# A matrix product with a decayed running sum: the first and last slots planned anew, chunk 2 read in pairs, the last two blocks copied in two pieces

## The chip, the cores and the metric

The kernel runs on one core of a Trainium2 chip, in one launch. Times are microseconds of device time (us): the median of several runs, and, for everything read from inside, one execution taken by the hardware profiler. The engines are named PE (matrix products), ACT (scalar engine), DVE (vector engine), POOL (GpSimd) and SP (the engine that issues the stores).

## The reference

```python
B, S, D = (16, 2048, 1024)          # x [B,S,D], w [D,D], decay [D], all float32
xw = x @ w
out[:, 0, :] = xw[:, 0, :]
for t in range(1, S):
    out[:, t, :] = decay[None, :] * out[:, t - 1, :] + xw[:, t, :]
```

Each of the 16 sequences is multiplied by one 1024x1024 matrix, and each output channel then runs a first-order recurrence over its 2048 time steps with its own decay.

## The kernel before

**Tiling.** Time is cut into 64 chunks of 512 tokens, four per sequence. The output channels are cut into eight blocks, n = 0 to 7, of 128. Chunks are taken two at a time; a *slot* is one pair of chunks and one n, so 31 pairs give 248 slots, and the last pair is split into its two chunks and gives 16 more: 264 slots. In a slot PE computes [128 channels x 1024 times] in PSUM with sixteen matmuls of 128x512 over the eight k-blocks (L131). Slots count from 0 and, near the end, backwards from -1. PSUM tiles come from a ring `ps` of three, so slot s writes the bank that slot s-3 used, and PE must wait until the readers of slot s-3 are done; two halves, `spare` and `spare1`, help at both ends.

**Input.** x is loaded by POOL's queue in four quarter loads for each chunk (`load`, L105, deed L) into `xb` (three buffers), cast to bf16 on the way. DVE transposes each chunk in 32x32 squares of float32 words (`turn`, L115, deed T), that is of pairs of bf16, into `xw` (two buffers). ACT then copies it in two parts (`part`, L123, deeds X and Y) into `xt`, where the even and odd members of the pairs are apart, and the matmuls read xt. Where the argument `pairs` is given, a matmul reads xw directly, every second bf16 of it, and needs no X or Y. A turn also puts the four loads of the chunk three further on in the list `loads`; each L in the plan issues the next one.

**Recurrence.** A slot is treated in one of two ways.
- *Direct*: DVE scans the 1024 times out of PSUM into `so` (`run`, L221, deed S).
- *Paired*: ACT copies PSUM to `xs` (L183, p), and writes the odd step's scaled value to `h` (L169 on ps, g); POOL adds them (`join`, L196, j); DVE scans only every second time, with the squared decay (L201, S); ACT scales those results (L169 on so, h), and POOL fills in the other times (`fill`, L246, c). z prepares the column ahead of the scan.

By default a slot is paired unless n % 4 == 3; `flips` lists the slots where this is turned round. k (L250) saves the last column for the next pair of chunks. DVE then transposes the slot back (`back`, L258, deed B) into an `ot` buffer, and when four blocks n are together, SP stores them in four stores (L279).

**The order.** `pin` keeps the program order on every engine, so the order in which the deeds are written is the order in which each engine works, and an engine whose next instruction has to wait holds up all behind it. For most slots `usual` makes the deeds. For the first slots (keys 0 to 33), and for the last (negative keys), the dictionary `agenda` has them written out, one line to a slot; the letters are the deeds above. Key -99 is done before the first slot: loads of x (M) and of w (U), transposes and copies of the first two chunks (E; F on DVE, G on ACT), and the weights' casts W on DVE and w on ACT (`settle`, L302). PE's own order is fixed by the loop over slots (L537). In slots 8 and 9 the matmuls of the two slots are issued chunk by chunk (L580 to L584).

**The end.** The last four slots are not transposed back by DVE. `ending` (L371, deed V) transposes them on PE in sixteen 128x128 pieces, blocks 0 to 3 of 128 times by rows r = 0 to 3 (L383), and `leave` copies each block of four rows from PSUM (L387; ACT for blocks 0 and 2, DVE for 1 and 3) and issues one store for it (L389).

Of the kernel before, what the change touches and what calls it, by code (L numbers as in the profile page):

```python
# [14 lines left out]
def _ap(ap_obj: bass.AP, new_ap, extra_offset=0):  # L15
    return dataclasses.replace(
        ap_obj,
        ap=[list(p) for p in new_ap],
        offset=ap_obj.offset + extra_offset,
    )  # L20
# [5 lines left out]
def kernel(  # L26
# [26 lines left out]
    nc = tc.nc  # L53
    pin = tc.keep_in_program_order
    B, S, D = x.shape
    assert w.shape == (D, D)

    NQ = 4
# [7 lines left out]
    R = K // 2  # L66
# [9 lines left out]
    def ring(pool, name, count, shape, dtype=FP32):  # L76
        i = turns[name] = turns.get(name, -1) + 1
        return pool.tile(shape, dtype, name=f"{name}{i % count}")
# [19 lines left out]
    xw_of = {}  # L98
# [42 lines left out]
    class Tile:  # L141
# [39 lines left out]
        def copy(self):  # L181
            self.xs = sb.tile([128, 2 * TL], FP32, name=f"xs{self.lot % 3}")[:, 0:self.T]
            pin(nc.scalar.copy(out=self.xs, in_=self.ps))  # L183
# [141 lines left out]
    for q in range(NQ):  # L325
        pin(nc.sync.dma_start(
            out=rows[q * P:q * P + R],
            in_=_ap(decay, [[P, R], [CH, 2], [1, P]], q * CR)))
# [42 lines left out]
    def ending(i):  # L371
        b, t0 = chunks[-1]
        nb = TL // 128
        pts = [ring(psp, name, count, [128, R, 128])
               for name, count in (("spare1", 1), ("ps", 3), ("ps", 3), ("spare", 1))]
        wides = [ring(sb, *spot, [128, NQ, R, P])
                 for spot in (("xb", 3), ("xb", 3), ("xb", 3), ("h", 4))]

        def cross(blocks, rs):
            for i in blocks:  # L380
                for r in rs:
                    t = 2 + i * 128
                    pin(nc.tensor.transpose(  # L383
                        out=pts[i][:, r], in_=tiles[r - R].so[:, t:t + 128], identity=ident))

        def leave(i, copy):
            pin(copy(out=wides[i].rearrange("p q r i -> p r q i"),  # L387
                     in_=pts[i].rearrange("p r (q i) -> p r q i", q=NQ)))
            pin(nc.sync.dma_start(  # L389
                out=_ap(out, [[D, 128], [1, CH]], (b * S + t0 + i * 128) * D + CH),  # L390
                in_=wides[i].rearrange("p q r i -> p (q r i)")))

        cross((0,), range(R))
        cross((1,), range(R))
        cross((2, 3), range(R - 1))
        cross((2, 3), (R - 1,))
        for i in range(nb):
            leave(i, (nc.scalar.copy, nc.vector.tensor_copy)[i % 2])

    slots = [(g, n) for g in groups[:-1] for n in range(K)]  # L400
    slots += [([c], n) for c in groups[-1] for n in range(K)]
    tiles = []

    def turn_and_load(c):
# [4 lines left out]
    loads = [(c, q) for c in (2, 3, 4) for q in range(NQ)]  # L409
# [19 lines left out]
        "d": square_again,  # L429
        "I": identity,  # L430
        "V": ending,
        "p": lambda s: tiles[s % len(slots)].copy(),
        "g": lambda s: tiles[s % len(slots)].odd(),
# [7 lines left out]
        "L": lambda i: load(*loads.pop(0)) if loads else None,  # L441
    }
    agenda = {
        -99: "M0 M1 U0 M2 M3 U1 U2 w0 W1 w2 W3 K0 K1 K2 K3 E0 E1 G0 E2 G1 E3 F2 G3 E4 E5 G4 E6 G5 E7 F6 G7 W4 w5 W6 W7 D E8 E9 G8 E10 G9 E11 F10 G11 E12 L E13 G12 L E14 G13 E15 L F14 G15",
        0: "p0 z0 W8 W9 W10 W11",
        1: "g0",
        2: "L S1 L",
        3: "p2 z2 L g2 j0 S3 w12 w13 L w14 L w15 k1",
        4: "j2 B1 d k3",
        5: "p4 L S0 L g4 S2 L k0 h0 j4 B3 h2",  # L450
        6: "k2 c0 T2 c2 p5 g5 B0 L X2 L",
        7: "B2 L L Y2 T3 L z4 z5 j5 p6 S4 z6 L g6 L X3 S5 j6 S7 Y3 L S6 h4 k7 k5 c4 k4 h5 B7",
        8: "",
        9: "k6 h6 c5 B4",
        10: "p8 g8 c6 T4 z8 p9 j8 g9 B5 X4",
        11: "L j9 B6 p10 S8 L z9 z10 g10 S9 h8",
        12: "j10 Y4 S11 L c8 h9 T5 c9",
        13: "p12 L g12 B9 j12 X5 S10 L",
        14: "Y5 B8 L B11 h10 z12 c10 S13",
        15: "p14 L g14 S12 j14 T6 h12 L",  # L460
        16: "p15 c12 g15 B10 L X6 j15 B12",
        17: "z14 Y6 S14 L B13 z15 h14 S15 p16 z16 c14",
        18: "g16 T7 L h15 j16 p17 g17 B14 z17 c15 X7",
        19: "S16 j17 p18 B15 L g18 L S17 k16 h16 z18 j18",
        20: "Y7 S19 L c16 k17 h17 T8 k19 L c17",
        21: "p20 g20 L S18 X8 j20 B17 B19",
        22: "L h18 p21 c18 B16 k18 g21 B18 Y8 z20 L j21 S20",
        23: "p22 z21 z22 S21 L h20 g22 T9 c20 h21",
        24: "k21 k20 j22 S23 X9 L c21 Y9 B20 L",
        25: "B23 k23 p24 B21 g24 z24 j24 S22 z25",  # L470
        26: "p25 T10 k22 h22 g25 c22 S24 X10 j25",
        27: "B22 p26 S25 g26 z26 Y10 j26",
        28: "S27 h25 h24 c25 S26 c24",
        29: "B27 h26 c26 T11 p28 g28 j28 B24",
        30: "p29 B25 g29 z28 j29 S28 z29 S29",
        31: "h28 p30 c28 B26 g30 h29 B28 j30 z30",
        32: "c29 S31 S30 h30 B29 c30 p32 g32 z32 j32 B30 B31 L L",
        33: "p33 g33 z33 j33 S32 h32 c32 k32 L L",
        -20: "z-20",
        -19: "p-20 g-20",  # L480
        -18: "j-20 S-19 S-20 k-19 B-19",
        -17: "h-20 k-20 c-20 S-18 B-20 k-18",
        -16: "I S-17",
        -15: "z-15 B-18 k-17",
        -14: "p-15 g-15 B-17 z-14 j-15",
        -13: "p-14 S-16 g-14 j-14 S-15 k-16",
        -12: "S-13 h-15 k-15 c-15 S-14 k-13",
        -11: "p-12 B-13 h-14 B-15 g-12 c-14 k-14 B-16",
        -10: "j-12 B-14 z-12 S-12 z-10 S-11",
        -9: "p-10 k-12 g-10 h-12 B-11 j-10 k-11",  # L490
        -8: "S-9 c-12 S-10 k-9",
        -7: "z-7 B-12 h-10 k-10 B-9 c-10 S-8",
        -6: "p-7 g-7 B-10 j-7 B-8",
        -5: "S-7 S-6 h-7 c-7",
        -4: "z-4 S-5 B-7",
        -3: "p-4 B-6 g-4 B-5 j-4",
        -2: "S-3 S-4",
        -1: "S-2 h-4 c-4 a-1 b-1 V",
    }
    flips = (1, 13, 15, -19, -18, -16, -11, -8, -6, -3, -2)  # L500
    later = {}
    begun = {"T": 12, "X": 11, "Y": 11}
    for c in range(5, nch):
# [6 lines left out]
    def usual(s):  # L510
# [9 lines left out]
        if not paired[s - 1]:  # L520
            do.append(f"B{s - 1}")
        return do + later.get(s, []) + ["L"] * (2 if len(loads) > NQ else 1)

    def rest(s):
        do = [f"S{s - 1}"] if tiles[s - 1].paired else []
        do.append(f"C{s - 1}")
        if tiles[s - 2].paired:
            do.append(f"B{s - 2}")
        return do + [f"B{s - 1}"] + later.get(s, []) + ["L"] * len(loads)

    def perform(do):
        for deed in do:
            deeds[deed[0]](int(deed[1:] or 0))
# [3 lines left out]
    for step, (g, n) in enumerate(slots):  # L537
        T = TL * len(g)
        left = step - len(slots)
# [5 lines left out]
        if step == 0:  # L545
# [10 lines left out]
            for k0 in range(0, K, 2):  # L556
                for i in range(R):
                    for k in (k0, k0 + 1):
                        matmul(seconds[i], i, k, xt_of[1], 0, H * P,
                               pairs=xw_of[1] if k0 < 4 else None)  # L560
            for i in range(R):
                for k in range(K):
                    matmul(seconds[i], i, k, xt_of[1], H * P, TL, H * P,
                           pairs=xw_of[1] if i < 2 else None)
        if step < R:
            ps = heads[n] if n < 3 else tuple(spares)
        else:
            if step == K + 1:
                ps = nexts
            elif len(g) == 2 or n % R < 3:  # L570
                ps = ring(psp, "ps", 3, [128, T])
            else:
                ps = ring(psp, "spare", 1, [128, TL])
            todo = [(k, l) for k in range(K) for l in range(len(g))]
            if step < K:
                todo.sort(key=lambda kl: kl[0] % 2)
            elif step == K:
                todo = []
                nexts = ring(psp, "ps", 3, [128, T])
                for l in range(len(g)):  # L580
                    for i, both in enumerate((ps, nexts)):
                        for k in range(K):
                            matmul(both[:, l * TL:(l + 1) * TL], n + i, k, xt_of.get(g[l]),
                                   pairs=xw_of[g[l]] if g[l] in (3,) else None)  # L584
            elif step == K + 1:
                todo = []
            if left == -1:
                ps = tuple(both[:, t:t + TL // 2] for t, both in zip(
                    (0, TL // 2), (ps, ring(psp, "ps", 3, [128, TL]))))
                for t, half in zip((0, TL // 2), ps):  # L590
                    for k in range(K):
                        matmul(half, n, k, xt_of[g[0]], t, t + TL // 2, t)
                todo = []
            for k, l in todo:
                matmul(ps[:, l * TL:(l + 1) * TL], n, k, xt_of[g[l]])
        tiles.append(Tile(g, n, ps, outlets))
        do = agenda.get(step, agenda.get(left) if left >= -20 else None)
        if do is None:
            do = usual(step)
        else:  # L600
            do = do.split()
            if left == -20:
                do = rest(step) + do
        perform(do)
    assert not loads
# [28 lines left out]
```

## Time and profile before

| what | value |
|---|---|
| median of 4 runs | 905.81 us (905.63 to 906.38) |
| profiled execution, whole | 905.67 us |
| its span in the profile | 903.80 us |
| granted TensorE clock | 0.999 |
| PE busy, share of the span | 896.6 us, 99% |
| DVE busy | 826.1 us, 91% |
| ACT busy | 684.4 us, 76% |
| POOL busy | 655.1 us, 72% |
| paired slots | 189 of 264 |
| memory read and written | 138.42 MB and 134.22 MB, 302 GB/s over the span |

The span runs from the first to the last instruction that the profiler shows; the execution's own time is 1.87 us longer. Starts and lengths below are from this one execution and count from the start of the span. A line of the timeline has start, length, engine, line of the kernel, operation and tiles, and in brackets the idle time before it with what ended it. "L131 <- DVE so L221" in a list of waits means that the matmul of line 131 waited for the instruction of line 221 on DVE.

### The profile page before, as it was taken

The page shows a single profiled execution, that of the slowest core. Times are in us where ns is not written, and L with a number is a line of the kernel's source. Part 1 is how long each engine was busy: PE and PEld are TensorE (multiplying, and loading weights), DVE is VectorE, ACT ScalarE, POOL GpSimd, SP SyncE. Part 2 cuts the span into 40 slices and gives each one's busy share as a digit, 9 for nine tenths or more (in the row PEclk, how much of TensorE's full clock was granted, in tenths as well). Part 3 has the DMA queues.
Part 4 walks back from the last instruction along what each step waited for, and adds up shares of the span by engine and source line. Part 5 has one row for each costly group of instructions (what it writes and reads, how often), then busy time and mean ns, then how long its engine had stood idle before and what let it go on. Part 6 is the DMA issues. An engine that isn't in the chain of part 4 may idle for free.

```text
span 903.8 us, 12070 instructions
## 1 busy us (share of the span) xinstructions
PE 896.6 (99%) x4201; PEld 411.2 (45%) x4201; DVE 826.1 (91%) x628; ACT 684.4 (76%) x951; POOL 655.1 (72%) x753
## 2 busy tenths in 40 slices
PE   9999999999999999999999999999999999999997
PEld 5444444444444444444444444444444444444444
DVE  4999999999999999999998999999999999999997
ACT  4889867777877877877778778778777787787742
POOL 7888678777767768677677677787777776776622
PEclk9999999999999999999999999999999999999999
DMA  9999999999999999999999999999999999999868
GB/s 193 195 215 218 231 214 216 215 240 251 238 247 258 242 247 257 250 243 243 225 236 229 223 229 232 227 228 229 228 229 225 236 231 223 225 233 209 175 143 233
DMA packets 402543, 204.77 MB, mean 227 GB/s; under 512 B 8753, under 2 KB 401457, under 8 KB 402481
## 3 DMA queue, kind: packets, MB, share of 16 engines
q1 hardware_dynamic: 265168, 134.76, 61.1%
q0 software_dynamic: 137024, 68.70, 56.7%
q8 instruction: 33, 0.54, 0.2%
q10 hardware_dynamic: 288, 0.52, 0.2%
q14 instruction: 30, 0.24, 0.1%
HBM read 138.42 MB, written 134.22 MB: 302 GB/s over the span
## 4 chain that ended last, share of the span: by engine, by line
PE 93%; DVE 2%; DMA 2%; POOL 2%; issue 1%; ACT 1%; DVEq 0%; POOLq 0%
PE ps L131 92%; DMA xb<-in_x_dram 2%; DVE so L221 1%; POOL ot L295 1%; PE spare L131 1%; POOL xb L105 1%; ACT xt L123 0%; DVE so L201 0%; ACT xs L183 0%; DVE ot L258 0%; DVE xw L115 0%; ACT h L169 0%; POOL xs L196 0%; PE spare L383 0%; PE ps L383 0%
## 5 line engine op out<-in xcount | busy, mean ns | idle before, releaser
L131 PE MATMUL ps<-xt,wsb 128*128 128x512 bf16 x4024 | 868.0, 378 | 0.9 <-DVE wsb L302 0.5
L131 PEld LDWEIGHTS <-wsb 128*128 128x128 bf16 x4152 | 405.9, 98 | 480.4 <-issue 1.0
L196 POOL TENSOR_TENSOR xs<-h,xs 128x512 f32<-128x512 f32 (+1 forms) x189 | 241.9, 1280 | 191.2 <-ACT h L169 84.1
L183 ACT COPY xs<-ps 128x1024 f32<-128x1024 f32 (+1 forms) x189 | 188.7, 998 | 155.3 <-PE ps L131 150.7
L258 DVE STREAM_TRANSPOSE ot<-so 128x1024 f32<-128x1024 f32 (+1 forms) x260 | 300.1, 1192 | 2.9 <-POOL so L190 1.1
L246 POOL TENSOR_TENSOR so<-h,xs 128x512 f32<-128x512 f32 (+1 forms) x189 | 240.3, 1273 | 43.3 <-ACT h L169 27.8
L123 ACT COPY xt<-xw 128x2048 bf16<-128x2048 bf16 (+1 forms) x136 | 242.2, 1789 | 7.7 <-DVE xw L115 7.7
L105 POOL DMA_DIRECT2D xb<-in_x_dram x264 | 174.0, 660 | 3.3 <-DMA ot<-in_w_dram 1.1
L169 ACT ACTIVATE h<-so,dec 128x512 f32<-128x512 f32 (+1 forms) x189 | 144.7, 766 | 26.8 <-DVE so L201 23.6
L115 DVE STREAM_TRANSPOSE xw<-xb 128x2048 f32<-128x2048 f32 (+1 forms) x78 | 147.3, 1901 | 5.6 <-DMA xb<-in_x_dram 5.6
L201 DVE TENSOR_TENSOR_SCAN so<-spare,keep,xs 128x512 f32<-128x512 f32 (+1 forms) x96 | 119.4, 1245 | 27.6 <-POOL xs L196 27.3
L201 DVE TENSOR_TENSOR_SCAN so<-spare,xs 128x512 f32<-128x512 f32 x93 | 113.3, 1220 | 26.7 <-POOL xs L196 23.8
L169 ACT ACTIVATE h<-ps,dec 128x512 f32<-128x512 f32 (+1 forms) x189 | 129.6, 685 | 0.0
L221 DVE TENSOR_TENSOR_SCAN so<-dec,ps 128x1024 f32<-128x1024 f32 x34 | 76.9, 2260 | 1.0 <-ACT h L169 1.0
L221 DVE TENSOR_TENSOR_SCAN so<-dec,keep,ps 128x1024 f32<-128x1024 f32 (+1 forms) x36 | 77.2, 2145 | 0.2
L250 ACT COPY keep<-so 128x1 f32<-128x1 f32 x136 | 25.4, 189 | 13.1 <-DVE so L221 12.6
L192 ACT COPY so<-keep 128x1 f32<-128x1 f32 x96 | 18.2, 191 | 2.0 <-DVE ot L258 1.8
L131 PE MATMUL ps<-xw,wsb 128*128 128x256 bf16 (+1 forms) x68 | 11.2, 301 | 0.0
L190 POOL MEMSET so<- 128x1 f32 x93 | 10.6, 116 | 0.6 <-DVE ot L258 0.6
L131 PE MATMUL spare<-xt,wsb 128*128 128x512 bf16 (+1 forms) x48 | 10.0, 335 | 0.0
L295 POOL DMA_DIRECT2D ot<-in_w_dram x12 | 6.5, 544 | 3.1 <-DMA xb<-in_x_dram 2.0
L320 PE MATMUL spare<-idle 128*128 128x512 bf16 x22 | 6.8, 484 | 1.2 <-DVE idle L310 1.2
(37 smaller groups left out, 36.5 us busy)
## 6 DMA issues: line engine op xcount, KB each, us to landing
out_dram<-ot SPq DMA_DIRECT2D x248, 512.0 KB, 11.0
xb<-in_x_dram POOLq DMA_DIRECT2D x248, 256.0 KB, 7.8
out_dram<-ot SPq DMA_DIRECT2D x12, 256.0 KB, 4.3
xb<-in_x_dram POOLq DMA_DIRECT2D x16, 128.0 KB, 5.6
ot<-in_w_dram POOLq DMA_DIRECT2D x12, 128.0 KB, 5.1
out_dram<-xb SPq DMA_DIRECT2D x3, 256.0 KB
ot<-in_w_dram ACTq DMA_DIRECT2D x2, 256.0 KB, 4.7
ot<-in_w_dram SPq DMA_DIRECT2D x2, 256.0 KB, 4.5
```

The source lines that it names most:

```text
L105: pin(nc.gpsimd.dma_start(out=xb_of[c][quad(q), j0:j1], in_=_ap(x, [[D, P], [P * D, j1 - j0], [1, CQ]], (b * S + t0 + j0 * P) * D + q * CQ)))
L115: pin(nc.vector.transpose(out=dst.rearrange("p (m j i) -> p j m i", m=M, i=P)[:, j0:j1, m0:m1], in_=src.rearrange("p (j m c) -> p j m c", ...
L123: pin(copy(out=xt_of[c][:, m0:m1, :, j0 * P:j1 * P], in_=src))
L131: pin(nc.tensor.matmul(out=ps[:, t0:t1] if ps.shape[1] >= t1 else ps, lhsT=lhs, rhs=rhs, start=(k == 0 and t0 == start), stop=(k == K - 1),))
L169: pin(nc.scalar.activation(out=h, in_=src, func=mybir.ActivationFunctionType.Copy, scale=dec[:, self.n:self.n + 1]))
L183: pin(nc.scalar.copy(out=self.xs, in_=self.ps))
L196: pin(nc.gpsimd.tensor_tensor(out=odds, in0=self.g, in1=odds, op=ALU.add))
L201: pin(nc.vector.tensor_tensor_scan(out=so[:, 3:T + 2:2], data0=squares[-1][:, n:n + 1].to_broadcast([128, T // 2]), data1=self.xs[:, 1:T:2 ...
L221: pin(nc.vector.tensor_tensor_scan(out=so[:, t + 2:t + 2 + size], data0=dec[:, n:n + 1].to_broadcast([128, size]), data1=ps, initial=befor ...
L246: pin(nc.gpsimd.tensor_tensor(out=self.so[:, 2:T + 2:2], in0=self.h, in1=self.xs[:, 0:T:2], op=ALU.add))
L250: pin(nc.scalar.copy(out=self.keep, in_=self.so[:, self.T + 1:self.T + 2]))
L258: pin(nc.vector.transpose(out=outlet.ot[:, :, c0:c0 + P], in_=self.so[:, 2 + t0:2 + t0 + nj * P].rearrange("p (i t) -> p i t", t=P)))
```

## The change

Four things are changed, and nothing in what is computed.
- The lines of `agenda` for slots 0 to 33 are written anew (32 and 33 stay), and so are those for the last slots, which now begin at -30 instead of -20; `rest`, which made the deeds ahead of the line -20, goes. In key -99 only the places of three loads L move behind the last deeds.
- `flips` is another list. Slot 0 is now direct and slot 13 paired, and so on; in all twelve more slots are paired (201 of 264). The squares W8, W9 and W11 of the weights are cast by ACT.
- In slots 8 and 9 the matmuls on chunk 2 read xw in pairs as those on chunk 3 did.
- `leave` takes a list of pieces. Blocks 2 and 3 are copied as rows 0 to 2 and row 3, in two instructions, with one store as before.

The diff, cut to the code and to the lines of the plan around the waits that the profile of before shows:

```diff
-        def leave(i, copy):
-            pin(copy(out=wides[i].rearrange("p q r i -> p r q i"),
-                     in_=pts[i].rearrange("p r (q i) -> p r q i", q=NQ)))
+        def leave(i, copy, pieces):
+            for r0, r1 in pieces:
+                pin(copy(out=wides[i].rearrange("p q r i -> p r q i")[:, r0:r1],
+                         in_=pts[i][:, r0:r1].rearrange("p r (q i) -> p r q i", q=NQ)))
...
-            leave(i, (nc.scalar.copy, nc.vector.tensor_copy)[i % 2])
+            leave(i, (nc.scalar.copy, nc.vector.tensor_copy)[i % 2],
+                  ((0, R),) if i < 2 else ((0, R - 1), (R - 1, R)))
...
-        -99: "M0 M1 [...] E12 L E13 G12 L E14 G13 E15 L F14 G15",
-        0: "p0 z0 W8 W9 W10 W11",
-        1: "g0",
-        2: "L S1 L",
-        3: "p2 z2 L g2 j0 S3 w12 w13 L w14 L w15 k1",
-        4: "j2 B1 d k3",
-        5: "p4 L S0 L g4 S2 L k0 h0 j4 B3 h2",
-        6: "k2 c0 T2 c2 p5 g5 B0 L X2 L",
-        7: "B2 L L Y2 T3 L z4 z5 j5 p6 S4 z6 L g6 L X3 S5 j6 S7 Y3 L S6 h4 k7 k5 c4 k4 h5 B7",
+        -99: "M0 M1 [...] E12 E13 G12 E14 G13 E15 F14 L G15",
+        0: "L L",
+        1: "S0 L",
+        2: "w9 L w8",
+        3: "L p2 W10 L B0 w11 w12 L S1 w13 z2 k0 w14 L w15",
+        4: "g2 S3 k1",
+        5: "L p4 j2 g4 z4 j4 B1 d k3 S2 L",
+        6: "p5 z5 L S4 g5 k2 h2 j5 B3 h4 c2 k4 T2",
+        7: "c4 p6 g6 S5 L X2 L B2 j6 T3 h5 z6 L Y2 c5 B4 L X3 L S7 L Y3 L S6",
         8: "",
-        9: "k6 h6 c5 B4",
-        10: "p8 g8 c6 T4 z8 p9 j8 g9 B5 X4",
-        11: "L j9 B6 p10 S8 L z9 z10 g10 S9 h8",
-        12: "j10 Y4 S11 L c8 h9 T5 c9",
+        9: "z8 k7 p8",
+        10: "B7 k6 g8 L T4 h6 j8 p9 c6 k5 g9",
+        11: "S8 X4 j9 B6 L Y4 B5 L",
+        12: "T5 z9 p10 L g10 z10 h8 j10 S9 X5 c8 S11",
...
-        -20: "z-20",
-        -19: "p-20 g-20",
-        -18: "j-20 S-19 S-20 k-19 B-19",
-        -17: "h-20 k-20 c-20 S-18 B-20 k-18",
-        -16: "I S-17",
-        -15: "z-15 B-18 k-17",
-        -14: "p-15 g-15 B-17 z-14 j-15",
+        -26: "z-26 p-27 T62 h-28 g-27 c-28 j-27 B-28 X62 L",
+        -25: "S-27 p-26 g-26 h-27 j-26 L",
+        -24: "z-24 S-25 Y62 c-27 S-26",
+        -23: "B-27 h-26 p-24 c-26 B-25 g-24 z-23 T63 j-24",
+        -22: "p-23 B-26 g-23 X63 j-23 S-24 z-22 S-23",
+        -21: "h-24 p-22 c-24 g-22 B-24 h-23 j-22 k-23 Y63",
+        -20: "c-23 S-21 k-24 z-20 S-22 k-21",
+        -19: "B-23 h-22 k-22 p-20 c-22 B-21 g-20 z-19 B-22 j-20 I",
+        -18: "p-19 z-18 S-20 g-19 h-20 j-19 k-20 c-20 S-19",
+        -17: "p-18 B-20 g-18 h-19 j-18 k-19 c-19 S-18",
+        -16: "z-16 S-17 k-18 h-18",
+        -15: "c-18 p-16 g-16 B-19 j-16 k-17",
+        -14: "p-15 g-15 S-16 z-15 j-15 B-18 h-16",
...
-    flips = (1, 13, 15, -19, -18, -16, -11, -8, -6, -3, -2)
+    flips = (0, 1, 15, 18, 19, 23, 25, 27, -7, -3, -2)
...
-                                   pairs=xw_of[g[l]] if g[l] in (3,) else None)
+                                   pairs=xw_of[g[l]] if g[l] in (2, 3) else None)
...
-        do = agenda.get(step, agenda.get(left) if left >= -20 else None)
+        do = agenda.get(step, agenda.get(left) if left >= -30 else None)
```

## The prediction

> **What bounds the kernel now.** I read the page's engine shares and its chain of waits first, then PE's waits, then PE's timeline around each wait, then the last 8 us. Span 903.80, profiled execution 905.67, so 1.87 us lie outside the span; the median of the runs shown is 905.81, 0.14 above this execution.
>
> ```profile
> PE 896.6 (99%) x4201; PEld 411.2 (45%) x4201; DVE 826.1 (91%) x628; ACT 684.4 (76%) x951; POOL 655.1 (72%) x753
> PE 93%; DVE 2%; DMA 2%; POOL 2%; issue 1%; ACT 1%; DVEq 0%; POOLq 0%
> ```
>
> PE is busy throughout and carries 93% of the chain. An edit pays only where PE stands still, or behind PE's last instruction. PE stands still here:
>
> ```profile
> PE spare L320 <- DVE idle L310: 1.2, 1, 1.2
> PE ps L131 <- DVE wsb L302: 0.5, 1, 0.5
> PE ps L131 <- ACT h L169: 0.3, 1, 0.3
> PE ps L131 <- DVE so L221: 0.2, 1, 0.2
> ```
>
> The first is ahead of all work and the second (14.88 us) waits for weights still landing; the change touches neither. The third is slot 9's first matmul, whose PSUM slot 6's odd scale (g6, L169) still reads; the fourth is slot -14 (14th from the end), whose bank slot -17's direct scan (L221) still reads:
>
> ```profile
> 40.82 0.38 PE L131 MATMUL ps<-xt,wsb 128*128 128x512 bf16 x1
> 41.48 1.89 PE L131 MATMUL ps<-xt,wsb 128*128 128x512 bf16 x8 [0.28 <-ACT h L169]
> 43.20 3.79 PE L131 MATMUL ps<-xw,wsb 128*128 128x512 bf16 x16
> ...
> 872.51 1.89 PE L131 MATMUL ps<-xt,wsb 128*128 128x512 bf16 x8 [0.17 <-DVE so L221]
> ```
>
> The columns are start, length, work and the gap ahead. The gap counts from the modelled end, but matmuls overlap: from 41.48 to 43.20 eight take 1.72, 0.215 each. So the third gap costs (41.48-40.82)-0.22 = 0.44, not 0.28 (0.22 is the spacing), and the fourth 0.17+0.38-0.22 = 0.33. Sixteen matmuls reading pairs (rhs xw) take 46.83-43.20 = 3.63, or 0.227 each.
>
> The end:
>
> ```profile
> 898.69 0.11 PE ps L383
> 898.80 0.12 PE spare L383
> 898.92 0.02 issue
> 898.95 0.69 DVE h L387
> ```
>
> and in the timeline of the same stretch:
>
> ```profile
> 898.25 1.62 SPq L389 DMA_DIRECT2D out_dram<-xb  x3
> ...
> 898.84 0.58 ACT L387 COPY xb<-ps 128x512 f32<-128x512 f32 x1 [0.61 <-PE ps L383]
> ...
> 899.96 0.40 SPq L389 DMA_DIRECT2D out_dram<-h  x1
> ```
>
> After the last transpose come two copies side by side, then SP issues one store behind the other: the third ends at 898.25+1.62 = 899.87, so the last goes at 899.96 though DVE was done at 899.64.
>
> **Part by part.** Matmul counts stay. Twelve more tiles are paired (copy, odd scale, join, half scan, even scale, fill instead of a direct scan); three weight copies go from DVE to ACT. By the rows, one such tile adds to ACT 1.0+0.69+0.77 and to POOL twice 1.28, and takes from DVE 2.26-1.22. These engines were at 76%, 72% and 91%, and only the ends of their chains reach PE, so I walked the new orders engine by engine with these durations, from the trace's starts.
>
> 1. *Stall at 41.2.* In the new line for slot 7, p6 and g6 stand ahead of part X2 on ACT; g6 ends near 38.5, and PE asks near 41.1. Gone: -0.44. Cover 2.6 us. Behind them on ACT queue X2, Y2, X3, Y3 (1.8 to 1.9 each, h5 between): X3 ends at 44.2, Y3 at 46.0; slot 10, the first to read them, starts at 39.31+32x0.227 = 46.6 and comes to Y3 eight matmuls later: 2.3 cover.
>
> 2. *Chunk 2 in pairs.* 16 x (0.227-0.215) = +0.18 (bounds 0 and 0.2). X2 and Y2 are then not needed by slots 8 and 9, but turn T2 is: it must end before slot 8, at 39.31. DVE runs S0 from 23.0, W10 25.2, B0 25.4, S1 26.5, S3 28.7 and 30.0, B1 31.2, S2 32.4, S4 33.5, B3 34.6, T2 35.7 to 38.0: 1.3 us of cover. T3 then ends at 42.4; its first pair matmul is due at 39.31+16x0.227 = 42.94: 0.5 cover.
> [...]
>
> 3. *The start's new order.* Slot 0 is now scanned directly: S0 ends at 25.27 for slot 4 due at 25.46; S1 ends at 28.81 for slot 5 due at 28.92; ACT's w9 w8 p2 w11 w12 w13 w14 w15 (0.52 each by L302's start-to-start) end at 28.50 for a need of 28.48. Cover 0.2, 0.1 and none: 0.02, bounded by 0 and 0.3 (at 862.44 a direct scan began 0.46 behind PE's matmul end; S0 starting so late would cost slot 4 that 0.3).
>
> 4. *T5 goes ahead of S9 and S11* on DVE (before: S11 at 55.12, T5 at 57.36). By the landings' spacing chunk 5 is there at 52.1; T5 starts at 53.6, T5 2.2 + S9 1.15 + S11 2.3 end at 59.4. Slot 14 wants S11's bank at 60.4: 1.0 cover, cost 0. T7 to T11 then run at the heels of their loads (starts 71.7, 81.8, 90.8, 101.1, 110.2; landings in before 71.75, 81.7, 91.4, 101.3, 111.1); DVE waits 0.1 to 0.9 each, and the slots behind keep 2.5 to 4 us: 0.
>
> 5. *The end's plan, slot -14.* It still waits for S-17, but ahead of it stand more paired tiles in a row. T63 starts at 848.95 as before; B-26 and S-24 follow, so S-24 ends at 853.5. From there, each step waiting for the last: h-24 0.78, c-24 1.29, B-24 1.13, S-21 2.18, S-22 1.22, h-22 0.78, p-20 0.91, g-20 0.69, j-20 1.30, S-20 1.23, h-20 0.78, p-18 0.91, g-18 0.69, j-18 1.30, S-18 1.23, S-17 2.26: 18.7, with 0.3 of handoffs 19.0. S-17 ends at 872.49 (before: 872.45) and PE goes 0.06 later, at 872.55. Without a stall PE asked at 872.18, now 0.26 sooner by steps 1 and 2: 871.92. The stall is 0.63 where it was 0.33: +0.30. If the whole chain moves with PE, the stall is 0.37 (+0.04); if the handoffs shrink by 0.05 each over 15, nothing is left (-0.33).
>
> 6. *Pieces.* The diff reads as if three rows were copied under the last transposes. In the built order only the first piece has a wait, and it counts to the last transposes (4200 of 4201 PE instructions for ACT's block, all for DVE's): nothing overlaps. A second instruction costs its fixed part. ACT copies 512 columns in 0.58 and 1024 in 1.01, so fixed 0.15, of which 0.11 overlaps its neighbour: +0.05. DVE's share, about 0.08, hides behind SP's third issue (0.2 cover). Sum +0.05; bounds 0 and 0.15.
> [...]
>
> Sum: -0.44+0.18+0.02+0.30+0.05 = +0.11. Profiled 905.78, median **905.9**.
>
> **Rivals.** *Slower: T5 late.* This plan issues POOL's loads later at the start: chunk 5's last at about 42.7, not 38.4. If a load lands by its issue and not by its place in the queue, this counts.
>
> ```profile
> DMA to landing us min/median/max: 8.2/10.9/13.7
> ```
>
> These are chunk 5's four loads (issued 36.49 to 38.39). With 13.7 the last lands at 56.4, T5 starts there, and S11 ends at 56.4+0.1+5.7 = 62.2 instead of 59.4, 1.8 late for slot 14: about 907.7, and one us more per us. It decides once T5 starts after 54.6. For: DVE has no gap from 40 to 60 in which to catch up. Against: chunks 5 to 11 landed evenly, 2.45 us a load, whenever issued, which is a full queue; it holds if it stays full.
>
> *A little faster.* The chain to S-17 is 0.6 shorter than I walk it, or the pieces do overlap (three rows copied while the last two transposes run, at most 0.35): 905.3 to 905.6; with both 905.1. For: the slack at slot -14 hangs on fifteen handoffs. Against: those in before are 0.04 to 0.13.
>
> *More than 1.8 us faster* would need more than all that PE loses in reach: 0.44+0.33 and some 0.5 of the tail.
>
> **How the numbers follow.** 0.2% of 905.81 is 1.81 us, about what a measurement of this kernel can tell from no change: 904.0 and 907.6. My sum as walked: 0.59. A little faster: 0.12. T5 late enough to pass 907.6, or several of the thin covers of steps 2 to 4 gone together with it: 0.26. Over 1.8 faster, by something no row shows: 0.03. So faster 0.03, same 0.71, slower 0.26. The range goes from both gains (905.1) to T5 late by half a us more than the rival's row (908.2). The forecast's own range is 905.5 to 906.6, by the bounds of steps 3, 5 and 6.
>
> **What would show it.** Right: PE's waits lose the ACT h L169 line; 32 matmuls with rhs xw in a row near 39 to 46; a gap near 872, put to DVE so L221, about 0.3 longer; two copies of the leave each on ACT and DVE behind the last transpose, with no matmul under them; L115 of chunks 7 to 11 waiting briefly for DMA xb. Wrong: a PE wait near 60 for DVE so L221 (the slower rival); none near 872, or copies starting before the last transpose (the gain); a PE wait at 25, 28 or 43 (a cover I read too wide); or a wait between 120 and 840, where the two orders are alike but for the tiles.

## The result and the profile after

| | before | after |
|---|---|---|
| median | 905.81 us (60 runs) | 906.94 us (42 runs) |
| ratio of after to before | | 1.0012 (95% interval 1.0008 to 1.0016) |
| profiled execution, its span | 905.67, 903.80 | 907.06, 905.28 |
| end of PE's last matmul | 898.91 | 898.83 |
| from there to the end of the span | 4.89 | 6.45 |

The change costs 1.1 us. That lies inside the range (905.1 to 908.2) and within 0.2% of no change, but 1.0 above the forecast of 905.9. It is also not where the sum looked: PE, which the sum followed, ends 0.08 *earlier*, and in the profiled execution all the time is lost behind its last matmul.

The engine shares hardly move (after: PE 99%, DVE 91%, ACT 77%, POOL 74%). The joins on POOL (L196) number 195, against 189 before: the change pairs six more slots (195 of 264), not the twelve (201) that the text ahead and the prediction say. No term of the sum was worked out from that count. PE's list of waits (us in total, times, longest), its last two lines:

```profile
PE ps L131 <- DVE wsb L302: 0.5, 1, 0.5
PE ps L131 <- DVE so L221: 0.3, 1, 0.3
```

The wait for ACT h L169 is gone, the one for DVE so L221 has grown. PE's timeline in the two places (start, length, work, gap ahead):

```profile
25.46 14.04 PE L131 MATMUL ps<-xt,wsb 128*128 128x512 bf16 x64
39.34 7.41 PE L131 MATMUL ps<-xw,wsb 128*128 128x512 bf16 x32
46.59 15.70 PE L131 MATMUL ps<-xt,wsb 128*128 128x512 bf16 x72
...
872.41 1.89 PE L131 MATMUL ps<-xt,wsb 128*128 128x512 bf16 x8 [0.32 <-DVE so L221]
```

Slot 10 starts at 46.59 instead of 46.83: 0.24 won at the start. Slot -14 starts at 872.41 instead of 872.51, so 0.14 of that is lost again there, and nothing in between. So far the chip does what the working says. The end of the timeline shows what it does not say; first SP's last issues and the copies:

```profile
898.17 2.35 SPq L390 DMA_DIRECT2D out_dram<-xb  x3
...
898.56 0.27 PE L383 MATMUL spare<-ident,so 128*128 128x128 f32 x1
898.76 0.65 ACT L388 COPY xb<-ps 128x384 f32<-128x384 f32 x2 [0.61 <-PE ps L383]
898.87 0.76 DVE L388 COPY h<-spare 128x384 f32<-128x384 f32 x2 [0.18 <-PE spare L383]
900.62 0.40 SPq L390 DMA_DIRECT2D out_dram<-h  x1
```

The copies end when they did before (899.41 and 899.63), in two pieces, both behind the last transpose of their block. But SP's three issues take 2.35 us, not 1.62, and the last store goes at 900.62, not 899.96. Before, each of the three took 0.35 to 0.39; now the first takes 1.09, the others 0.35 and 0.40. The first stands behind the stores of slots -8 to -5, which SP was still issuing until 897.46. That SP is held up by the stores ahead in its queue is a reading so far; it is tested below. What had still to be written from 900 on, by the DMA view of the window 900 to 906, before and then after:

```profile
DMA packets 425, 0.77 MB, mean 129 GB/s; under 512 B 51, under 2 KB 51, under 8 KB 424
```

```profile
DMA packets 638, 1.07 MB, mean 178 GB/s; under 512 B 73, under 2 KB 136, under 8 KB 637
```

0.3 MB more, at the 360 GB/s of 900 to 902, is an estimated 0.8 us, about half of the 1.56 by which the tail grew in this one execution. Where the 0.3 MB come from stands 25 us earlier. DVE from slot -17's scan on, in before:

```profile
870.20 2.25 DVE L221 TENSOR_TENSOR_SCAN so<-dec,ps 128x1024 f32<-128x1024 f32 x1
872.38 2.34 DVE L258 STREAM_TRANSPOSE ot<-so 128x1024 f32<-128x1024 f32 x2
```

and in after:

```profile
870.10 2.26 DVE L221 TENSOR_TENSOR_SCAN so<-dec,ps 128x1024 f32<-128x1024 f32 x1
872.28 1.22 DVE L258 STREAM_TRANSPOSE ot<-so 128x1024 f32<-128x1024 f32 x1
873.42 0.71 DVE L201 TENSOR_TENSOR_SCAN so<-spare,keep,xs 128x256 f32<-128x256 f32 x1
874.05 2.94 DVE L258 STREAM_TRANSPOSE ot<-so 128x1024 f32<-128x1024 f32 x3
```

S-17 ends at about the same time (872.45 and 872.36). But before, two transposes back stood behind it (B-18, B-17), and now three (B-19, B-18, B-17) with S-16 between them. The four stores of slots -20 to -17, 2 MB, go when the last of the four is transposed (in before B-17 ends at 874.72 and the first store starts at 874.74). SP's line in the windows from 874, before and after:

```profile
874.74 10.53 SPq L279 DMA_DIRECT2D out_dram<-ot  x6
```

```profile
876.42 8.39 SPq L279 DMA_DIRECT2D out_dram<-ot  x5
```

They start 1.68 us later. In windows of two us (columns: PE, PEld, DVE, ACT, POOL busy, clock, DMA share, GB/s) before shows the DMA engines nearly idle at 874 to 876 and with some room again at 894 to 896; after shows them nearly idle until 878, and from 880 on busy at 0.89 or more in every window up to 902:

```profile
874.00:876.00 2.00, 2.00 (x11) 0.92 (x10) 2.00 (x3) 1.05 (x3) 0.89 (x2) 1.00 0.16 35
876.00:878.00 2.00, 2.00 (x11) 0.94 (x10) 2.00 (x3) 0.96 (x5) 0.94 (x2) 1.00 0.84 176
...
894.00:896.00 2.00, 2.00 (x16) 1.34 (x14) 2.00 (x3) 0.53 (x1) 0.00 (x0) 1.00 0.84 152
```

```profile
874.00:876.00 2.00, 2.00 (x11) 0.90 (x10) 2.00 (x3) 1.55 (x5) 1.28 (x3) 1.00 0.22 58
876.00:878.00 2.00, 2.00 (x11) 0.88 (x9) 2.00 (x4) 0.54 (x3) 0.51 (x1) 1.00 0.27 63
...
894.00:896.00 2.00, 2.00 (x16) 1.41 (x15) 2.00 (x3) 0.53 (x1) 0.03 (x1) 1.00 0.96 226
```

So the theory to be tested: **the late stores of slots -20 to -17 leave a backlog of data still to be written; PE's end does not wait for it, but the end of the program does.** Its rivals are the pieces of the last copies, and the new start with its later loads.

### The profile page after: what moved, and what is told of

Read it like the earlier page. It is cut to its first block, busy times and chain, and to the rows that moved or that the text cites. A ratio compares the mean times of both kernels' runs of the same rounds, so it can differ in the third digit from the quotient of the medians.

```text
span 905.3 us, 12116 instructions
## 1 busy us (share of the span) xinstructions
PE 896.2 (99%) x4201; PEld 411.0 (45%) x4201; DVE 821.3 (91%) x626; ACT 696.1 (77%) x977; POOL 667.3 (74%) x767
## 5 line engine op out<-in xcount | busy, mean ns | idle before, releaser
L196 POOL TENSOR_TENSOR xs<-h,xs 128x512 f32<-128x512 f32 (+1 forms) x195 | 247.8, 1271 | 181.6 <-ACT h L169 78.3
L183 ACT COPY xs<-ps 128x1024 f32<-128x1024 f32 (+1 forms) x195 | 193.7, 993 | 147.3 <-PE ps L131 142.4
L246 POOL TENSOR_TENSOR so<-h,xs 128x512 f32<-128x512 f32 (+1 forms) x195 | 246.5, 1265 | 39.2 <-ACT h L169 28.0
L169 ACT ACTIVATE h<-so,dec 128x512 f32<-128x512 f32 (+1 forms) x195 | 148.8, 764 | 26.7 <-DVE so L201 23.5
L201 DVE TENSOR_TENSOR_SCAN so<-spare,keep,xs 128x512 f32<-128x512 f32 (+1 forms) x100 | 122.6, 1229 | 28.9 <-POOL xs L196 28.4
L169 ACT ACTIVATE h<-ps,dec 128x512 f32<-128x512 f32 (+1 forms) x195 | 133.3, 684 | 0.0
L221 DVE TENSOR_TENSOR_SCAN so<-dec,ps 128x1024 f32<-128x1024 f32 x32 | 72.3, 2260 | 1.3 <-PE ps L131 1.3
L221 DVE TENSOR_TENSOR_SCAN so<-dec,keep,ps 128x1024 f32<-128x1024 f32 (+1 forms) x32 | 71.0, 2220 | 0.0
L131 PE MATMUL ps<-xw,wsb 128*128 128x256 bf16 (+1 forms) x84 | 14.8, 317 | 0.0
```

Of the source, the lines that this page charges most:

```text
L131: pin(nc.tensor.matmul(out=ps[:, t0:t1] if ps.shape[1] >= t1 else ps, lhsT=lhs, rhs=rhs, start=(k == 0 and t0 == start), stop=(k == K - 1),))
L169: pin(nc.scalar.activation(out=h, in_=src, func=mybir.ActivationFunctionType.Copy, scale=dec[:, self.n:self.n + 1]))
L196: pin(nc.gpsimd.tensor_tensor(out=odds, in0=self.g, in1=odds, op=ALU.add))
L201: pin(nc.vector.tensor_tensor_scan(out=so[:, 3:T + 2:2], data0=squares[-1][:, n:n + 1].to_broadcast([128, T // 2]), data1=self.xs[:, 1:T:2 ...
L221: pin(nc.vector.tensor_tensor_scan(out=so[:, t + 2:t + 2 + size], data0=dec[:, n:n + 1].to_broadcast([128, size]), data1=ps, initial=befor ...
L246: pin(nc.gpsimd.tensor_tensor(out=self.so[:, 2:T + 2:2], in0=self.h, in1=self.xs[:, 0:T:2], op=ALU.add))
```

## Experiments

Each median stands beside that of the kernel before on the same chip. Intervals are some 0.0009 (0.8 us) to either side, so a single comparison shows a direction at best; the theory rests on several that agree, and on the traces. "Tail" is the time from the end of PE's last matmul to the end of the span in the profiled execution: 4.9 for before, 6.45 for after.

| kernel | median | before | ratio (95% interval) | tail |
|---|---|---|---|---|
| after, whole copies | 907.04 | 905.99 | 1.0009 (1.0000 to 1.0018) | 5.7 |
| new start alone | 905.37 | 905.99 | 0.9993 (0.9984 to 1.0002) | 4.9 |
| the same again | 905.39 | 906.02 | 0.9994 (0.9986 to 1.0003) | 4.9 |
| new end alone | 907.24 | 905.99 | 1.0014 (1.0005 to 1.0022) | 5.8 |
| before, B-17 late | 907.15 | 905.99 | 1.0012 (1.0003 to 1.0021) | 6.0 |
| before, pieces | 905.82 | 906.02 | 0.9999 (0.9990 to 1.0008) | 5.3 |
| after, 4 stores left out | 906.44 | 906.02 | 1.0005 (0.9997 to 1.0014) | 5.6 |
| before, 4 stores left out | 906.10 | 906.02 | 1.0001 (0.9992 to 1.0010) | 5.2 |
| after, B-18 and B-17 early | 907.95 | 906.02 | 1.0021 (1.0013 to 1.0030) | 5.5 |
| new start, S-17 early | 905.86 | 906.02 | 1.0000 (0.9991 to 1.0009) | 4.9 |
| the same again | 905.65 | 906.02 | 0.9995 (0.9986 to 1.0004) | 5.0 |
| the same, ACT's store queue | 916.26 | 906.02 | 1.0114 (1.0100 to 1.0128) | 16.4 |

**The parts of the change.** Whole copies again in the kernel after:

```diff
-                  ((0, R),) if i < 2 else ((0, R - 1), (R - 1, R)))
+                  ((0, R),))
```

> The kernel after, with blocks 2 and 3 copied whole again. Store theory (the end is set by the store queue, whose four stores of slots -20 to -17 were issued 1.7 us later than before, 876.42 against 874.74, and which then never runs empty again): the pieces cost 0.05 at most, so 906.9 as the kernel after, with last stores as late. Pieces theory (the second copies hold up SP, whose longest store issue at the end went from 0.39 to 1.09 us): 906.2 to 906.3, and the last store issued near 900.0 instead of 900.62.

907.04, no less than after, and SP's three issues are as slow as there (from 898.55, 2.37 us). The pieces do not hold up SP. The other way round, the kernel before with pieces:

```diff
-            leave(i, (nc.scalar.copy, nc.vector.tensor_copy)[i % 2])
+            leave(i, (nc.scalar.copy, nc.vector.tensor_copy)[i % 2],
+                  ((0, R),) if i < 2 else ((0, R - 1), (R - 1, R)))
```

> The kernel before with blocks 2 and 3 copied in two pieces, nothing else changed. By the sum of the prediction 0.05 more: 905.85 to 905.95. If a piece costs what the two kernels without the stores of slots -20 to -17 differ by (0.34): 906.1 to 906.3.

905.82 against 906.02: the pieces cost nothing that can be measured, and they gain nothing. The profiled tails of the kernels with pieces are 0.4 to 0.8 longer than those of their counterparts without (6.45 against 5.7, 5.3 against 4.9, and 5.6 against 5.2 without the four stores). The medians of the first two pairs do not confirm it.

The new start alone: the lines of `agenda` from 0 on, key -99, the flips from 0 on and the pairs of after; the end's lines, flips and copies of before.

```diff
-    flips = (0, 1, 15, 18, 19, 23, 25, 27, -7, -3, -2)
+    flips = (0, 1, 15, 18, 19, 23, 25, 27, -19, -18, -16, -11, -8, -6, -3, -2)
...
-        -30: "z-30 X61 Y61 L",
...
+        -20: "z-20",
```

> The new start and the pairs of chunk 2, with the end's plan and the copies of before. Store theory: PE comes to the end 0.25 us sooner and the stores of slots -20 to -17 go at 874.5 to 874.7, so 905.4 to 905.8. If the new start, with its later loads, were what costs time: 906.5 or more.

> The new start with the end of before once more, beside the next kernel on one chip. Its PE comes 0.25 sooner by the start, and the earlier start of slot -14's stall: 905.4 to 905.8.

905.37 and 905.39, 0.6 below the kernel before beside them, twice. The start with its later loads costs nothing, it gains. Each interval still holds 1.0, so a gain of 0.6 is what two comparisons agree on and neither proves. In the second one's trace PE has no wait left from 26 us to the last slots:

```profile
59.70 814.72 PE L131 MATMUL ps<-xt,wsb 128*128 128x512 bf16 x3699
```

The 0.33 wait of slot -14 is absent, although S-17 stands where it stood (870.18, 2.25 long): in this execution PE came to its first matmuls on xt 0.6 later than in the trace of before, and used the slack up by itself. So a part of what PE loses at the start is given back there, and that part of a gain at the start is lost there.

The new end alone (the other half of the same edit, with whole copies):

```diff
-    flips = (1, 13, 15, -19, -18, -16, -11, -8, -6, -3, -2)
+    flips = (1, 13, 15, -7, -3, -2)
...
+        -30: "z-30 X61 Y61 L",
```

> The start of before, with the new end's plan and whole copies. Store theory: the stores of slots -20 to -17 go 1.7 to 2 us later than in the kernel before and PE gains nothing at the start, so 906.9 to 907.2. If the start or the pieces were what costs time: 905.8 to 906.0.

907.24. The whole loss is in the end's plan. SP's issue of the four stores starts at 876.71, and its last three issues take 2.16. The parts (start -0.6, pieces 0, end +1.25) make +0.6, and the whole is +1.1; with intervals of 0.8 us to either side that is no contradiction. On one chip and with whole copies, the new start is worth 0.2 beside the new end (907.04 against 907.24) and 0.6 beside the old (905.37 against 905.99). That what PE wins at the start does not reach the end when the stores set it would explain this; it is not shown.

**The suspected cost alone.** The kernel before, with one transpose back moved behind two scans; slots, pairs, start and copies stay:

```diff
-        -14: "p-15 g-15 B-17 z-14 j-15",
-        -13: "p-14 S-16 g-14 j-14 S-15 k-16",
+        -14: "p-15 g-15 z-14 j-15",
+        -13: "p-14 S-16 g-14 j-14 S-15 k-16 B-17",
```

> The kernel before with one transpose back moved: B-17 stands behind S-16 and S-15 on DVE, so the four stores of slots -20 to -17 start 1.8 us later, and nothing else is changed. Store theory: PE's end stays within 0.1 us, yet the last store lands 0.9 to 1.5 later: 906.7 to 907.3. If the end hangs on PE's last instruction and the copies alone: 905.8.

907.15, +1.16: the loss of the whole change from one delayed transpose. SP and its last issues in this trace:

```profile
876.88 8.56 SPq L279 DMA_DIRECT2D out_dram<-ot  x5
```

```profile
898.58 2.26 SPq L389 DMA_DIRECT2D out_dram<-xb  x3
900.94 0.57 SPq L389 DMA_DIRECT2D out_dram<-h  x1
```

The stores go 2.1 later than in before; 0.3 of that is a later start of this execution (first matmul on xt at 15.20 against 14.88), and PE's end is later by that much and no more (899.24 against 898.91). So PE lost nothing, and still the program ends 1.2 later. For the data left, executions are best compared from PE's end: from 1.09 us behind its last matmul on, the time 900 in before, the DMA view has 0.77 MB left in before, 1.09 in after, 1.04 here, 1.03 and 0.97 in the two other kernels with late stores (after with whole copies, new end alone), and 0.77 in both executions of the new start alone. This is the run that shows the mechanism. The edit moves little else: S-16 and S-15, for which B-17 makes room, start 1.1 sooner, and the DVE work behind them some 0.2 later, both counted from PE's first matmuls on xt.

**The stores taken away.** Both kernels without the four stores of slots -20 to -17:

```diff
-                if not outlet.missing:
+                if not outlet.missing and not -20 <= self.turn - len(slots) <= -17:
```

> The kernel after without the four stores of slots -20 to -17 (their 2 MB of the output are not written; all else is done). Store theory: with these 2 MB gone the queue has room again behind 876, so the time falls by 1.2 to 1.9 us, to 905.0 to 905.7, and comes within 0.4 of the kernel before without the same stores. If the pieces or PE carried the loss, the two would still be 1.0 or more apart.

> The kernel before without the four stores of slots -20 to -17 (their 2 MB are not written). Store theory: its queue ran nearly dry at 891 to 893 as it is, so little is to be gained, 0.2 to 0.8: 905.0 to 905.6. If stores play no part at the end: 905.8 as before.

906.44 and 906.10. The two come within 0.34 of each other, from 1.1, as expected. But neither falls as far as expected: before gains nothing, so it had no backlog left at its end, and the 0.2 to 0.8 that I allowed it were wrong; the time of after falls by about 0.5, not 1.2 to 1.9, and the intervals of its two ratios (1.0012 and 1.0005) overlap. The trace is clearer than the median. In after without the four stores:

```profile
898.26 1.59 SPq L390 DMA_DIRECT2D out_dram<-xb  x3
```

```profile
DMA packets 443, 0.78 MB, mean 130 GB/s; under 512 B 53, under 2 KB 71, under 8 KB 442
```

SP's three issues are as short as in before (1.62; 2.35 in after), and the data left from 900 on is that of before (0.77 MB; 1.07 in after), with PE's end at 898.92. So the hold-up of SP and the 0.3 MB do come from the four stores. Under the backlog lies a floor of some 4.9 to 5.6 us from PE's last matmul: copies, issues and 1 MB of the last four stores. The remaining 0.34 is inside the intervals and stays open; the pieces, which after has and before has not, are not excluded as its cause.

**Attempts to mend the end.** In after, B-18 and B-17 ahead of S-16:

```diff
-        -14: "p-15 g-15 S-16 z-15 j-15 B-18 h-16",
-        -13: "k-16 p-14 c-16 B-17 g-14 z-14 j-14",
+        -14: "p-15 g-15 z-15 j-15 B-18 B-17 S-16 h-16",
+        -13: "k-16 p-14 c-16 g-14 z-14 j-14",
```

> The kernel after with B-18 and B-17 ahead of S-16 on DVE, so that the stores of slots -20 to -17 go 0.65 us sooner (near 875.75). Store theory: 0.4 to 0.7 less, 906.2 to 906.5. If their time does not matter: 906.9.

907.95, slower by another 1.0: a miss, and no test of the theory. The stores did start sooner (876.03 against 876.42), but S-16 later pushed the whole chain of the last slots on, and PE's transposes waited for it, in the list of PE's waits from 890 on:

```profile
PE spare L383 <- POOL so L246: 1.3, 1, 1.3
```

PE's last matmul ends at 900.71 there. Next, on the new start with the end of before, S-17 ahead of B-20, to free slot -14's bank sooner:

```diff
-        -17: "h-20 k-20 c-20 S-18 B-20 k-18",
-        -16: "I S-17",
+        -17: "h-20 k-20 c-20 S-18 k-18",
+        -16: "I S-17 B-20",
```

> The new start with the end of before (start_only), and S-17 ahead of B-20 on DVE, so that slot -14 finds its bank free; B-17 and the stores behind it end as before. The wait for DVE so L221 near 872 goes and PE ends 0.33 sooner. If PE's end sets the time: 905.0 to 905.1 against 905.37 of start_only. If the store queue sets it there too: 905.3 to 905.4, no change.

> The same with S-17 ahead of B-20, once more. From PE's end to the last packet it took 3.61 us, start_only 3.58 and before 3.64, so there the end hangs on PE's end and not on a backlog; the wait near 872 being gone, 0.1 to 0.3 less than start_only: 905.2 to 905.5.

905.86 and 905.65: no gain over the new start alone (905.37, 905.39), which has no wait left to lose there. Whether it costs 0.3 stays open; the intervals hold both. Last, ACT issuing two of the last four stores:

```diff
-            pin(nc.sync.dma_start(
+            pin((nc.scalar, nc.sync)[i % 2].dma_start(
                 out=_ap(out, [[D, 128], [1, CH]], (b * S + t0 + i * 128) * D + CH),
```

> As start_swap, and the stores of blocks 0 and 2 are issued by ACT behind its own copies instead of by SP, so that the stores of blocks 1 and 3 go straight behind DVE's copies (898.8 and 899.7 instead of 899.18 and 900.14 on the clock of start_swap's trace). If SP's serial issue sets the last landing: 0.25 to 0.4 less than start_swap, 904.9 to 905.2. If the rate at which the last megabyte is written sets it: no change, 905.2 to 905.5.

916.26, ten us slower, for a reason that neither side of the expectation thought of. In the windows of its trace (DMA share and GB/s last) the DMA engines stand still while PE runs:

```profile
890.00:892.00 2.00, 2.00 (x10) 0.91 (x10) 2.00 (x4) 0.57 (x2) 0.40 (x1) 1.00 0.00 0
892.00:898.00 6.00, 6.00 (x42) 3.96 (x40) 5.82 (x8) 1.50 (x4) 1.47 (x2) 1.00 0.01 3
```

SP issues nothing from 887.04 to 900.10, though the data of slots -12 to -9 was in `ot` by 888.4. It goes on 2.1 us behind the issue of ACT's first store (897.98). What SP waited for the trace does not name; the program built for this run does. There the stores take eight completion counters in turn, and the wait of each is for the count that the one before it on its counter brings. ACT's two stores have their turns ahead of SP's last sixteen; the first of SP's stores to come round to the same counter is the first of slots -12 to -9, and nine more stand behind it. So SP stood, by this reading, until ACT's first store had landed, and this run says nothing about SP's serial issue.

The fastest kernel run is the new start with the end of before (905.37 and 905.39); as said, neither interval excludes that it equals before.

## Why the prediction was right or wrong

- *What bounds it.* Right for PE's span, and incomplete for the rest. The last eight us were read as a chain of copies and issues; that the DMA engines behind them had little room was in the windows of before (DMA share 0.84 to 0.99 between 890 and 896) and was not used.
- *Step 1*, the stall at 41.2, and *step 2*, the pairs: right. -0.26 was worked out, -0.24 measured at slot 10; the 32 pair matmuls take 46.59-39.34 = 7.25, or 0.227 each, as the row said. No run shows step 2's lower bound of 0: a matmul that read pairs took 0.227 in before and in after, one that read xt 0.215 in before.
- *Steps 3 and 4*, the thin covers: all held. T5 starts at 53.51 (53.6 worked out) and S11 ends at 59.19 (59.4); T7 to T11 start 0.7 to 1.7 later than walked, and PE does not notice. The slower rival, T5 late, did not happen, although a load issued between 38 and 46 took up to 16.0 us to land.
- *Step 5*, slot -14. S-17 ends at 872.36 (872.49 worked out), and the stall is 0.32+0.38-0.22 = 0.48 (0.63 worked out). Right for PE, but **this is also the step that failed:** it followed S-17 only to the bank that PE waits for. Behind S-17 on DVE the new plan has B-19, S-16, B-18 and B-17 where the old had B-18 and B-17, and with B-17 go four stores. I named who waits for S-17 and not who waits for what is queued behind it. The runs put that term at 1.2 (B-17 late alone), the size of the whole loss.
- *Step 6*, the pieces: right that they do not overlap, and +0.05 is below what the medians resolve (+1.05 for after without them, -0.2 for before with them); in the trace two pieces take 0.65 on ACT and 0.76 on DVE, where one copy took 0.58 and 0.69, so +0.07 each. But the sum of +0.05 for the tail took the last store's landing as fixed behind its issue; the tail measured +1.56 in the profiled execution.
- *The gain and the rivals.* The gain case failed: no overlap, and a chain to S-17 that was 0.13 shorter than walked, not 0.6. The time of 906.94 lies outside the forecast's own range (905.5 to 906.6, by the bounds of steps 3, 5 and 6); the wide range held only because it reached to 908.2 for a slower rival that did not happen. That is luck: the loss came from a cause that no rival names.
- *Part by part.* "Twelve more tiles" should be six; the count stands in no term.

## What to carry to other kernels

In this kernel the DMA engines were 0.84 to 1.04 busy in every window of two us from 876 to 902 in before and from 880 to 902 in after, and the program's end followed PE's end by 4.9 us only as long as the stores kept up: with 0.77 MB still to be written 1.09 us behind PE's last matmul the tail was 4.9 (before), with 1.04 MB it was 6.0 (B-17 late alone), though PE lost nothing. So in a plan that ends like this one, follow each moved instruction to the *stores* that it releases, and compare the megabytes still to be written at PE's end, not only PE's own waits. The chain of waits did not show this: it ends at DVE's last copy, at 899.64 in before and 899.63 in after, while data was written until 902.5 and 903.8. The new start was worth 0.6 beside the old end and 0.2 beside the new one, with intervals of 0.8 to either side; whether a gain at the start and a loss at the end add up is not shown, and the parts of a plan that was changed in two places are worth running alone.

## What was not expected of the hardware

Stores by rows of 512 bytes ran at 216 to 271 GB/s (before, 880 to 894), those of the last four, mostly by rows of 2 KB, at 371 (before) and 359 (after) at 900 to 902, with the DMA engines busy nearly all the time in both. Whether it matters that the compute engines stand still at the end is not separated: in the run with ACT's store queue they stood still at 900 to 902 too, and 219 GB/s were moved there at a DMA share of 0.86. Of four stores issued together, SP's first issue took 0.32 us, the third and fourth 2.15 and 2.63 (before, from 874.74 on). Moving two stores to another engine's queue cost 10 us (916.26 against 905.86 and 905.65): SP issued nothing from 887.04 to 900.10, and the DMA engines stood idle meanwhile (0.00 to 0.01 busy from 890 to 898).
